# Pooling on token slices, and the next weights split behind the norms, in a two-layer encoder trunk on one core

## The chip, the cores and the metric

The kernel runs on one NeuronCore of a Trainium2 chip. TensorE (PE in the profile; PEld is its weight load) multiplies, VectorE (DVE), ScalarE (ACT) and GpSimd (POOL) work element by element, SyncE (SP) issues most of the transfers. The metric is the device time of one execution in microseconds; lower is better.

## The reference

528 tokens (16 learned meta tokens and 512 frames) of 1024 channels pass through two layers. Each layer is a half-step SwiGLU FFN, a token mixer and another half-step FFN, all with an RMS norm in front and a residual around. The mixer of the first layer is pooling, that of the second is latent attention.

```python
h = h + 0.5 * swiglu(rmsnorm(h, ffn1_norm[l]), ffn1_w_gate[l], ffn1_w_up[l], ffn1_w_down[l])
u = rmsnorm(h, mix_norm[l])
h = h + pool_mixer(u, pool_w[l], pool_scale[l])        # first layer
...
def pool_mixer(h, w_group, scale):
    # per group of 256 channels: mean over the last w tokens (w = 2, 4, 8, 16) minus the token,
    # then a 256 x 256 map per group, then a scale per channel
def swiglu(h, w_gate, w_up, w_down):
    return (jax.nn.silu(h @ w_gate) * (h @ w_up)) @ w_down     # 1024 -> 2816 -> 1024
```

All data is float32.

## The kernel before

**Layout.** Channels lie on the partitions: `h` is eight tiles of 128 channels by 528 tokens. Every product is made in three passes of a reduced-precision float format: an operand is split into a high part (ScalarE copies it) and a low part (VectorE subtracts the copy), and high x high, high x low and low x high are added up in PSUM. So each operand, weights too, costs one ScalarE and one VectorE instruction before TensorE can use it.

**Weights.** `fetch(u)` (line 162) brings one unit of 128 x 1024 into one of two buffers (`raw`) by SyncE's queue, copies it (L169) and subtracts (L170); `fetch_gate_up` (line 331) does so for the gate and the up unit of one chunk. `wide` tiles hold the parts, 14 of them.

**FFN.** The 2816 hidden channels are 22 chunks of 128. A *plain* chunk (`gate_up_plain`, `plain`, L371) is 8 k-tiles x 3 passes x 2 token halves x 2 (gate and up) = 96 matmuls. A *recursive* chunk (`gate_up`, `product`, L383) gets gate and up from 7 products of half the depth, 84 matmuls, out of sums of the weights and sums of the inputs. The weight sums are brought by `bring_sums` (two SyncE transfers and one accumulating GpSimd transfer, L401 to L403) and `bring`, added and split by `prepare` (L421, L422, L183, L184). The input sums are made by `sums_x(x, k)` (L245 to L248, then L183 and L184), one call for each pair of k-tiles. The first chunks of an FFN are plain: in the first, second and fourth FFN `first_chunks` runs five (`begun = 5`), in the third `first_chunk` runs two. Down products (L193) of a block of four chunks are handed out over the slots of the next block.

**Norms at an FFN's start.** In `first_chunks` chunk 0 and 1 are made from inputs that lack the norm's factor. `rms[0]()` makes the factor's columns, `rms[1]()` spreads them over the partitions (L303) and ScalarE copies them out (L307, L305). Then `normal_x` for each of eight k-tiles multiplies (L224, VectorE), copies the high part (L183, ScalarE) and subtracts (L184, VectorE). Chunk 2 takes the k-tiles one after the other (`by_chunk`). In the third FFN the inputs are normalised in the stage before it, between the products of the shared keys and values, and handed over as `x_1`.

**Pooling.** After the first FFN the residual `h` of a channel tile is written by VectorE (L617), split into `xm` (L210 ScalarE, L211 VectorE), squared (L262) and the square added to a running sum (L263, GpSimd mostly). `z_products` (L734) multiplies token tiles by the group's weights; `z_scale` makes the norm's factor per token, `z_parts` (L740, L741) scales and splits; band matrices then do the pooling over tokens (L766 to L778), L780 adds the residual, and the next FFN's input is split and squared. A band product over 256 or 272 output tokens needs earlier tokens too. Four token tiles are slices of 128; the tokens left over, 240 to 255 and 512 to 527, are gathered by GpSimd copies (L695) into a fifth tile of 80 rows (`x5`, `s5`), which has zeros between.

**Order.** The order of instructions on each engine is set when the kernel is built, by a planner that goes by the order of the program, by what is ready, and by estimated durations. An engine then works its list in order. `with tc.issue_after(i):` adds one constraint: instructions written inside the block for the engine of `i` come after `i` on that engine. Instructions of other engines are not bound.

Of the kernel before, what the change touches and what calls it, by code (L numbers as in the profile page):

```python
# [58 lines left out]
B_0, B_4, B_M, NB = 0, 256, 528, 928  # L59
# [21 lines left out]


def tail(ap):

    return ap.rearrange("p (a b) -> p a b", b=NM)[:, 15::17, :]


def spread(ap):

    return ap.rearrange("p (a b) -> p a b", b=64)[:, :, :NM]  # L90
# [3 lines left out]
def trunk(ctx: ExitStack, tc, h0, wall, vecs, band, rope, out):  # L94
# [24 lines left out]
    def unsplit():  # L119
        return rawp.tile([P, 1024], F32, tag="raw", name=name("raw"))  # L120

# [59 lines left out]
    def split_to(dst, src):  # L181

        nc.scalar.activation(dst[0], src, AF.Copy)  # L183
        nc.vector.tensor_tensor(dst[1], src, dst[0], op=ALU.subtract)  # L184
# [33 lines left out]
    def normal_x(xs, c, g, t0, r):  # L218
# [6 lines left out]
        if c >= KC // 2:  # L225
            p = slot(F32R)[:, :T], slot(F32R)[:, :T]
            split_to(p, xn)
            xs["b"][c] = [(p[0][:, a : a + n], p[1][:, a : a + n]) for a in (0, n)]
            return
# [101 lines left out]
    def fetch_gate_up(u0, one=fetch):  # L331
        one(u0)
        one(u0 + 1)

    def ffn(u0, x, g, rms, t0, after, early=None, final=None, normed=None, hooks=()):
# [56 lines left out]

        def pair_of_sums():
            return sump.tile([P, 2, 512], F32, tag="sum", name=name("sum"))
# [136 lines left out]
        def first_chunks():  # L531

            nonlocal x
# [16 lines left out]
            plain(w_g, pg, halves)  # L550
            r = rms[1]()
            fetch_gate_up(u0 + 6)
# [6 lines left out]
            fetch_gate_up(u0 + 9)  # L559
            sums_x(x, 0)  # L560
            gate_up_plain(2, True)
            fetch_gate_up(u0 + 12)
            sums_x(x, 1)
            sums_x(x, 2)
            gate_up_plain(3)
            bring_sums(5)
            bring(5)
            evacuate(0, *held, r)
            sums_x(x, 3)
            bring_sums(6)  # L570
            gate_up_plain(4, pair=True)
            prepare(5)
            bring(6)

        def first_chunk():
# [6 lines left out]
            for k in range(2):  # L582
                sums_x(x, k)
            gate_up_plain(1)
            for k in range(2, 4):
                sums_x(x, k)
            prepare(2)
# [38 lines left out]
        begun = 5 if normed is None else 2  # L626
# [42 lines left out]
    rows = [P, P, P, P, 80]  # L669
    x5, bands = [], []  # L670

    def early():
# [11 lines left out]
        for i in range(2):  # L684
            x5.append((slot(F32R)[:, :512], slot(F32R)[:, :512]))
            for t in x5[i]:
                nc.gpsimd.memset(t.bitcast(F32), 0.0)

    done = prep([(xm, V_MIX, 0)], ssq_m, 0)

    def after(c):
        done(c)
        for e in range(2):
            t = x5[c // 4][e][:, (c % 4) * P : (c % 4) * P + P]
            nc.gpsimd.tensor_copy(spread(t), tail(xm[c][e]))  # L695
# [5 lines left out]
    s5 = slot()[:, :P]  # L701
    nc.gpsimd.memset(s5, 0.0)
    nc.vector.tensor_copy(spread(s5), tail(ssq_m))

    def tokens(j, c, e):
        if j == 4:
            return x5[c // 4][e][:, (c % 4) * P : (c % 4) * P + 80]
        return xm[c][e][:, j * P : (j + 1) * P]

    def z_scale():  # L710

        ps = psum()
        for j in range(5):
            sj = s5[:, :80] if j == 4 else ssq_m[:, j * P : (j + 1) * P]
            nc.tensor.matmul(ps[: rows[j], 2 * j : 2 * j + 2], sj, ones_d, start=True, stop=True)
        v, rc = small(5), small(5)
        nc.vector.memset(v, 1.0)
        nc.vector.tensor_scalar(v[:, :4], ps[:, 0:8:2], EPS, None, op0=ALU.add)
        nc.vector.tensor_scalar(v[:80, 4:5], ps[:80, 8:9], EPS, None, op0=ALU.add)
# [17 lines left out]
    def z_parts(j, b, ps):  # L737
# [3 lines left out]
        nc.vector.scalar_tensor_tensor(zl, ps, rc[:n, j : j + 1], zh, op0=ALU.mult, op1=ALU.subtract)  # L741
        z[j][b] = zh, zl

# [7 lines left out]
    for j, b in ((1, 1), (2, 1), (3, 1), (4, 1)):  # L751
        z_parts(j, b, z_products(j, b, psum()))
# [530 lines left out]
```

## Time and profile before

| | |
|---|---|
| time, three runs | 1695.87, 1699.82, 1700.03 us (median 1699.82) |
| profiled execution | 1702.0 us, of which the profile's span is 1700.2 |
| mean granted clock of TensorE | 0.981 of full speed |
| busy, share of the span | TensorE 96%, VectorE 67%, ScalarE 48%, GpSimd 13% |
| matmuls | 11976 |

How to read it: a row of the timeline is an instruction (or several alike, x count) with its start, its duration, engine, line of the code, operation and shape; in square brackets stands how long the engine stood idle before it and what ended that. Durations of neighbours on one engine can overlap by some hundredths of a microsecond; the chain shows net times. Matmuls overlap by more, so their pitch is the length of a run of them over their count.

### The profile page before, as it was taken

The numbers are of one execution on the slowest core, as the hardware profiler recorded it, in microseconds if no ns is written. First come the engines' busy times: TensorE is split into PE (matmuls) and PEld (weight loads), VectorE is DVE, ScalarE is ACT, GpSimd is POOL, SyncE is SP. The second block draws the span as 40 slices with busy tenths as digits, with TensorE's granted clock in tenths as the row PEclk, the third lists the DMA queues.
The fourth block names the chain that finished last, engine by engine and source line by source line (L and its number), as shares of the span: only waits on it lengthen the run. The fifth ranks groups of instructions, "written<-read, shape, count | busy, mean of one in ns | idle before, by whom it ended". The sixth has DMA issues, their size and how long they took to land.

```text
span 1700.2 us, 30059 instructions
## 1 busy us (share of the span) xinstructions
PE 1637.3 (96%) x11976; PEld 1555.5 (91%) x11976; DVE 1142.5 (67%) x1851; ACT 809.5 (48%) x1489; POOL 221.9 (13%) x257
## 2 busy tenths in 40 slices
PE   7999999998999999999899999999899899999997
PEld 7899999997999999999899999898787798999897
DVE  6865666657776566657767667566787766666655
ACT  6543444446454444445454444445576453444443
POOL 2000000005200000002000000001454100000002
PEclk9999999997999999999999999999899899999998
DMA  7455465533244555534355565643102434565411
GB/s 250 112 137 149 139 160 139 141 111 109 75 113 137 148 146 136 138 101 149 88 135 150 153 145 152 152 126 111 50 14 75 124 96 132 142 160 148 134 56 61
DMA packets 166206, 212.20 MB, mean 125 GB/s; under 512 B 10288, under 2 KB 102576, under 8 KB 166064
## 3 DMA queue, kind: packets, MB, share of 16 engines
q1 hardware_dynamic: 146176, 172.60, 32.2%
q0 software_dynamic: 19312, 37.23, 13.3%
q8 instruction: 94, 1.54, 0.4%
q10 hardware_dynamic: 576, 0.43, 0.1%
q14 instruction: 48, 0.39, 0.1%
HBM read 208.12 MB, written 2.10 MB: 124 GB/s over the span
## 4 chain that ended last, share of the span: by engine, by line
PE 84%; DVE 8%; DMA 3%; ACT 3%; issue 1%; POOL 0%; SPq 0%; DVEq 0%; ACTq 0%; POOLq 0%
PE ps L383 41%; PE ps L193 32%; PE ps L371 7%; DMA raw<-wall 2%; DVE t L184 2%; DVE t L224 1%; DVE w L170 1%; PE ps L1065 1%; DMA half<-wall 1%; ACT w L183 1%; DVE w L184 1%; PE ps L978 1%; PE ps L734 0%; PE ps L933 0%; ACT t L990 0%
## 5 line engine op out<-in xcount | busy, mean ns | idle before, releaser
L383 PE MATMUL ps<-t,w 128*128 128x256 f32 (+1 forms) x5964 | 757.1, 283 | 7.9 <-ACT t L525 6.7
L383 PEld LDWEIGHTS ps<-t,w 128*128 128x128 f32 x5964 | 740.1, 188 | 21.0 <-ACT t L525 8.1
L193 PE MATMUL ps<-t,w 128*128 128x264 f32 (+2 forms) x3672 | 628.4, 322 | 6.6 <-ACT t L183 2.0
L193 PEld LDWEIGHTS ps<-t,w 128*128 128x128 f32 x3672 | 527.9, 188 | 54.3 <-ACT t L183 5.0
L183 ACT ACTIVATE w<-half 128x512 fp32r<-128x512 f32 (+1 forms) x263 | 154.6, 603 | 230.8 <-PE ps L383 122.4
L371 PE MATMUL ps<-t,w 128*128 128x264 f32 (+1 forms) x1632 | 222.0, 297 | 21.5 <-DVE t L184 10.1
L371 PEld LDWEIGHTS ps<-t,w 128*128 128x128 f32 x1632 | 211.7, 199 | 30.1 <-DVE t L184 15.0
L403 POOL DMA_DIRECT2D sum<-wall x71 | 86.2, 1215 | 1077.9 <-DMA sum<-wall 400.6
L183 ACT ACTIVATE w<-sum 128x1024 fp32r<-128x1024 f32 x142 | 149.9, 1057 | 161.1 <-PE ps L383 108.2
L184 DVE TENSOR_TENSOR w<-half,w 128x512 fp32r<-128x512 f32 (+1 forms) x263 | 168.4, 655 | 70.6 <-ACT w L183 69.0
L184 DVE TENSOR_TENSOR w<-sum,w 128x1024 fp32r<-128x1024 f32 x142 | 173.1, 1220 | 54.3 <-PE ps L383 36.8
L614 DVE SCALAR_TENSOR_TENSOR h<-ps,h 128x528 f32<-128x528 f32 (+1 forms) x160 | 111.6, 697 | 140.1 <-PE ps L193 139.8
L183 ACT ACTIVATE t<-t 128x528 fp32r<-128x528 f32 (+4 forms) x174 | 99.0, 593 | 115.8 <-DVE t L526 62.9
L521 DVE TENSOR_TENSOR t<-ps,t 128x256 f32<-128x256 f32 (+1 forms) x71 | 30.3, 427 | 139.4 <-PE ps L383 138.5
L184 DVE TENSOR_TENSOR t<-t,t 128x528 fp32r<-128x528 f32 (+4 forms) x174 | 109.3, 643 | 11.2 <-ACT t L183 9.9
L184 DVE TENSOR_TENSOR w<-raw,w 128x1024 fp32r<-128x1024 f32 x71 | 86.7, 1221 | 28.1 <-PE ps L383 20.5
L183 ACT ACTIVATE w<-raw 128x1024 fp32r<-128x1024 f32 x71 | 74.9, 1055 | 55.5 <-PE ps L383 26.0
L170 DVE TENSOR_TENSOR w<-raw,w 128x1024 fp32r<-128x1024 f32 (+1 forms) x52 | 67.3, 1297 | 22.7 <-ACT w L169 21.1
L169 ACT ACTIVATE w<-raw 128x1024 fp32r<-128x1024 f32 (+1 forms) x55 | 54.5, 994 | 54.3 <-DMA raw<-wall 23.1
L263 POOL TENSOR_TENSOR t<-t,t 128x528 f32<-128x528 f32 (+1 forms) x33 | 52.9, 1603 | 156.4 <-ACT t L262 99.1
L513 ACT ACTIVATE t<-ps 128x256 f32<-128x256 f32 (+1 forms) x71 | 27.3, 385 | 81.8 <-PE ps L383 81.2
L211 DVE SCALAR_TENSOR_TENSOR t<-h,vt,t 128x528 fp32r<-128x528 f32 (+1 forms) x48 | 52.2, 1107 | 6.3 <-ACT t L210 6.1
(167 smaller groups left out, 1080.5 us busy)
## 6 DMA issues: line engine op xcount, KB each, us to landing
raw<-wall SPq DMA_DIRECT2D x118, 512.0 KB, 3.4
half<-wall SPq DMA_DIRECT2D x199, 256.0 KB, 3.8
sum<-wall SPq DMA_DIRECT2D x142, 256.0 KB, 3.2
sum<-wall POOLq DMA_DIRECT2D x71, 512.0 KB, 7.0
half<-wall SPq DMA_DIRECT2D x64, 192.0 KB, 2.8
h<-h SPq DMA_DIRECT2D x8, 264.0 KB, 5.6
raw<-wall SPq DMA_DIRECT2D x8, 256.0 KB, 4.0
raw<-band SPq DMA_DIRECT2D x4, 464.0 KB, 4.1
```

The source lines that it names most:

```text
L169: nc.scalar.activation(wh[:, a:b], raw[:, a:b], AF.Copy)
L170: low.tensor_tensor(wl[:, a:b], raw[:, a:b], wh[:, a:b], op=ALU.subtract)
L183: nc.scalar.activation(dst[0], src, AF.Copy)
L184: nc.vector.tensor_tensor(dst[1], src, dst[0], op=ALU.subtract)
L193: nc.tensor.matmul(ps, w[a], x[b][:, c0:c1], start=first and n == 0, stop=last and n == 2)
L211: nc.vector.scalar_tensor_tensor(xl, src, gain(g + c), xh, op0=ALU.mult, op1=ALU.subtract)
L263: (nc.vector if last else nc.gpsimd).tensor_tensor(ssq, ssq, sq, op=ALU.add)
L371: nc.tensor.matmul(ps, w[a][:, k * P : k * P + P], xs[k][i][b], start=k == 0 and n == 0, stop=k == KC - 1 and n == 2,)
L383: nc.tensor.matmul(ps, w[a][:, k * P : k * P + P], xs[k][b], start=first and k == 0 and n == 0, stop=last and k == 3 and n == 2, skip_grou ...
L403: nc.gpsimd.dma_start(t, up[:, :512].unsqueeze(1).to_broadcast([P, 2, 512]), accum_op=ALU.add)
L521: add(u[:, first], pd, u[:, first], op=ALU.add)
L614: nc.vector.scalar_tensor_tensor(hv, at, 0.5, hv, op0=ALU.mult, op1=ALU.add)
```

## The change

Pooling uses five slices of the token axis, 0 to 128, 128 to 256, 240 to 368, 368 to 496 and 496 to 528, with no gathered tile: the fifth has 32 rows, the copies, zeroed tiles and `s5` go, and the band matrices are 16 columns wider. The two fetches for the second FFN's first chunk are written inside a block behind the last low part of z. In `first_chunks` the factor is spread after six of the eight k-tiles of chunk 1's gate, the weights and input sums from chunk 3 on are written behind the low part of the last norm, and six chunks are plain instead of five (`begun = 6`). In `first_chunk` (third FFN) the sums and `prepare(2)` are written behind the last norm.

```diff
-B_0, B_4, B_M, NB = 0, 256, 528, 928
+B_0, B_4, B_M, NB = 0, 256, 528, 944
...
     def split_to(dst, src):
 
-        nc.scalar.activation(dst[0], src, AF.Copy)
-        nc.vector.tensor_tensor(dst[1], src, dst[0], op=ALU.subtract)
+        return (
+            nc.scalar.activation(dst[0], src, AF.Copy),
+            nc.vector.tensor_tensor(dst[1], src, dst[0], op=ALU.subtract),
+        )
...
-            split_to(p, xn)
+            _, xs["low"] = split_to(p, xn)
...
-            plain(w_g, pg, halves)
+            plain(w_g, pg, halves, range(6))
             r = rms[1]()
+            plain(w_g, pg, halves, range(6, KC))
             fetch_gate_up(u0 + 6)
             xs = new_x()
             for c in range(KC):
...
             x = xs
-            fetch_gate_up(u0 + 9)
-            sums_x(x, 0)
-            gate_up_plain(2, True)
-            fetch_gate_up(u0 + 12)
-            sums_x(x, 1)
-            sums_x(x, 2)
-            gate_up_plain(3)
-            bring_sums(5)
-            bring(5)
-            evacuate(0, *held, r)
-            sums_x(x, 3)
-            bring_sums(6)
-            gate_up_plain(4, pair=True)
-            prepare(5)
-            bring(6)
+            with tc.issue_after(xs["low"].ins):
+                fetch_gate_up(u0 + 9)
+                sums_x(x, 0)
+                gate_up_plain(2, True)
+                fetch_gate_up(u0 + 12)
+                sums_x(x, 1)
+                sums_x(x, 2)
+                gate_up_plain(3)
+                fetch_gate_up(u0 + 15)
+                sums_x(x, 3)
+                gate_up_plain(4)
+                evacuate(0, *held, r)
+                bring_sums(6)
+                bring(6)
+                bring_sums(7)
+                gate_up_plain(5, pair=True)
+                prepare(6)
+                bring(7)
...
             bring_sums(2)
             bring(2)
-            for k in range(2):
-                sums_x(x, k)
-            gate_up_plain(1)
-            for k in range(2, 4):
-                sums_x(x, k)
-            prepare(2)
+            with tc.issue_after(x["low"].ins):
+                for k in range(2):
+                    sums_x(x, k)
+                gate_up_plain(1)
+                for k in range(2, 4):
+                    sums_x(x, k)
+                prepare(2)
...
-        begun = 5 if normed is None else 2
+        begun = 6 if normed is None else 2
...
-    rows = [P, P, P, P, 80]
-    x5, bands = [], []
+    spans = [(0, P), (P, 2 * P), (240, 368), (368, 496), (496, L)]
+    rows = [b - a for a, b in spans]
+    bands = []
...
-        for i in range(2):
-            x5.append((slot(F32R)[:, :512], slot(F32R)[:, :512]))
-            for t in x5[i]:
-                nc.gpsimd.memset(t.bitcast(F32), 0.0)
-
-    done = prep([(xm, V_MIX, 0)], ssq_m, 0)
-
-    def after(c):
-        done(c)
-        for e in range(2):
-            t = x5[c // 4][e][:, (c % 4) * P : (c % 4) * P + P]
-            nc.gpsimd.tensor_copy(spread(t), tail(xm[c][e]))
+
+    after = prep([(xm, V_MIX, 0)], ssq_m, 0)
...
-    s5 = slot()[:, :P]
-    nc.gpsimd.memset(s5, 0.0)
-    nc.vector.tensor_copy(spread(s5), tail(ssq_m))
-
     def tokens(j, c, e):
-        if j == 4:
-            return x5[c // 4][e][:, (c % 4) * P : (c % 4) * P + 80]
-        return xm[c][e][:, j * P : (j + 1) * P]
+        return xm[c][e][:, slice(*spans[j])]
...
     for j, b in ((1, 1), (2, 1), (3, 1), (4, 1)):
-        z_parts(j, b, z_products(j, b, psum()))
-
-    fetch(U_FFN2_0, 2)
-    fetch(U_FFN2_0 + 1, 2)
+        low = z_parts(j, b, z_products(j, b, psum()))
+
+    with tc.issue_after(low.ins):
+        fetch(U_FFN2_0, 2)
+        fetch(U_FFN2_0 + 1, 2)
...
-        b_2, b_3 = bm[:, P : P + 272], bm[:, :272]
-        b_4 = b04[:80, B_4 : B_4 + 272]
+        b_2, b_3 = bm[:, P + 16 : P + 288], bm[:, 16:288]
+        b_4 = b04[: rows[4], B_4 : B_4 + 272]
...
-        b[:, g, B_M : B_M + 400] = entries(s, np.arange(-P, 272)[None], w, True)
-        src = np.full(P, -1000)
-        src[:16] = np.arange(240, 256)
-        src[64:80] = np.arange(512, 528)
-        b[:, g, B_4 : B_4 + 272] = entries(src[:, None], np.arange(256, 528)[None], w, True)
+        b[:, g, B_M : B_M + 416] = entries(s, np.arange(-P, 288)[None], w, True)
+        b[:, g, B_4 : B_4 + 272] = entries(s + 496, np.arange(256, 528)[None], w, True)
```

## Rows read from the trace of the kernel before

**Rows 1.** The page's first part: busy time, share of the span, instructions.

```profile
PE 1637.3 (96%) x11976; PEld 1555.5 (91%) x11976; DVE 1142.5 (67%) x1851; ACT 809.5 (48%) x1489; POOL 221.9 (13%) x257
```

**Rows 2.** Stretches: length, each engine's busy time (instructions), granted clock, DMA share, GB/s.

```profile
37.76:61.74 23.98, 18.86 (x112) 17.02 (x113) 22.67 (x46) 11.93 (x19) 1.24 (x1) 0.86 0.47 133
382.65:418.20 35.55, 27.55 (x166) 25.71 (x167) 27.52 (x36) 20.43 (x32) 20.43 (x25) 0.76 0.36 115
448.92:491.35 42.43, 41.92 (x338) 41.23 (x338) 39.20 (x72) 20.73 (x39) 2.44 (x2) 1.00 0.36 88
817.53:839.57 22.04, 16.85 (x103) 15.04 (x102) 21.97 (x48) 7.89 (x19) 1.23 (x1) 0.85 0.29 73
1342.44:1357.98 15.54, 11.08 (x45) 8.10 (x45) 15.54 (x35) 6.25 (x13) 0.00 (x0) 0.74 0.45 102
```

**Rows 3.** Timeline of TensorE in two undisturbed stretches of plain matmuls.

```profile
466.91 24.60 PE L371 MATMUL ps<-t,w 128*128 128x264 f32 x200 [0.23 <-DVE t L184]
...
1316.65 11.49 PE L371 MATMUL ps<-t,w 128*128 128x256 f32 x96
```

**Rows 4.** The chain that ended last, 40 to 60 us: start, net us, what.

```profile
39.67 0.68 DVE t L184 x2
40.35 0.68 DVE t L224
...
43.88 1.13 DVE w L170
...
49.76 0.34 DVE t L247
```

**Rows 5.** VectorE's groups by shape, 33.95 to 56.6 us: busy, mean ns | idle before.

```profile
L170 DVE TENSOR_TENSOR w<-raw,w 128x1024 fp32r<-128x1024 f32 x4 | 4.9, 1221 | 2.6 <-ACT w L169 2.6
...
L245 DVE TENSOR_TENSOR t<-t 128x264 f32<-128x264 f32 x4 | 1.7, 425 | 0.0
```

**Rows 6.** Timeline of the first FFN's start, ScalarE, and its first recursive products.

```profile
32.68 0.58 ACT L307 ACTIVATE t<-ps 128x512 f32<-128x512 f32 x1
...
34.95 1.06 ACT L169 ACTIVATE w<-raw 128x1024 fp32r<-128x1024 f32 x1 [1.62 <-DMA raw<-wall]
35.92 0.72 ACT L183 ACTIVATE t<-t 128x264 fp32r<-128x264 f32 x2
...
82.79 11.85 PE L383 MATMUL ps<-t,w 128*128 128x264 f32 x96
```

**Rows 7.** Timeline of the fourth FFN's start, ScalarE and VectorE.

```profile
1336.82 0.60 ACT L307 ACTIVATE t<-ps 128x512 f32<-128x512 f32 x1
...
1339.15 0.69 DVE L421 TENSOR_TENSOR sum<-sum,raw 128x512 f32<-128x512 f32 x1 [3.45 <-DMA raw<-wall]
...
1341.62 1.41 DVE L224 SCALAR_TENSOR_TENSOR t<-h,vt,t 128x512 f32<-128x512 f32 x2
```

**Rows 8.** Timeline of the third FFN's start, VectorE and ScalarE.

```profile
816.89 2.35 DVE L184 TENSOR_TENSOR w<-sum,w 128x1024 fp32r<-128x1024 f32 x2
...
817.51 0.57 ACT L307 ACTIVATE t<-ps 128x512 f32<-128x512 f32 x1
```

**Rows 9.** VectorE's and GpSimd's groups by shape, about 382 to 418 us.

```profile
L211 DVE SCALAR_TENSOR_TENSOR t<-h,vt,t 128x528 fp32r<-128x528 f32 x8 | 8.6, 1093 | 1.3 <-ACT t L210 1.3
L170 DVE TENSOR_TENSOR w<-raw,w 128x1024 fp32r<-128x1024 f32 x4 | 6.7, 1678 | 0.3 <-ACT w L169 0.3
...
L695 POOL CAST t<-t 128x32 fp32r<-128x32 f32 x16 | 10.3, 658 | 21.9 <-ACT t L210 19.7 <-DVE t L211 2.1
```

**Rows 10.** The chain that ended last, 380 to 420 us.

```profile
391.00 3.32 DMA raw<-wall
...
394.42 1.06 ACT w L169
```

**Rows 11.** Timeline of VectorE in the band loop.

```profile
422.80 0.75 DVE L211 SCALAR_TENSOR_TENSOR t<-h,vt,t 128x528 fp32r<-128x528 f32 x1
...
430.95 0.88 DVE L780 SCALAR_TENSOR_TENSOR h<-ps,vt,h 128x256 f32<-128x256 f32 x2
```

More of the change, by code (lines that the diff above doesn't have):

```diff
@@ L80 @@
 """
[L83 to L90, printed above, removed]
 @with_exitstack
@@ L120, in unsplit, with pair_of_sums @@
         return rawp.tile([P, 1024], F32, tag="raw", name=name("raw"))
+    def pair_of_sums():
+        return sump.tile([P, 2, 512], F32, tag="sum", name=name("sum"))
     def psum():
@@ L328, in prep, with fetch_gate_up @@
         return after
-    def fetch_gate_up(u0, one=fetch):
-        one(u0)
-        one(u0 + 1)
+    def fetch_gate_up(u0):
+        fetch(u0)
+        fetch(u0 + 1)
     def ffn(u0, x, g, rms, t0, after, early=None, final=None, normed=None, hooks=()):
@@ L390, in product @@
                     )
-        def pair_of_sums():
-            return sump.tile([P, 2, 512], F32, tag="sum", name=name("sum"))
         def bring_sums(f):
@@ L713, in z_scale @@
         for j in range(5):
-            sj = s5[:, :80] if j == 4 else ssq_m[:, j * P : (j + 1) * P]
-            nc.tensor.matmul(ps[: rows[j], 2 * j : 2 * j + 2], sj, ones_d, start=True, stop=True)
-        v, rc = small(5), small(5)
+            nc.tensor.matmul(ps[: rows[j], 2 * j : 2 * j + 2], ssq_m[:, slice(*spans[j])], ones_d, start=True, stop=True)
+        v, rc, n = small(5), small(5), rows[4]
         nc.vector.memset(v, 1.0)
         nc.vector.tensor_scalar(v[:, :4], ps[:, 0:8:2], EPS, None, op0=ALU.add)
-        nc.vector.tensor_scalar(v[:80, 4:5], ps[:80, 8:9], EPS, None, op0=ALU.add)
+        nc.vector.tensor_scalar(v[:n, 4:5], ps[:n, 8:9], EPS, None, op0=ALU.add)
         for a, b in ((0, 2), (2, 5)):
@@ L740, in z_parts @@
         nc.scalar.activation(zh, ps, AF.Copy, scale=rc[:n, j : j + 1])
-        nc.vector.scalar_tensor_tensor(zl, ps, rc[:n, j : j + 1], zh, op0=ALU.mult, op1=ALU.subtract)
+        low = nc.vector.scalar_tensor_tensor(zl, ps, rc[:n, j : j + 1], zh, op0=ALU.mult, op1=ALU.subtract)
         z[j][b] = zh, zl
+        return low
     two = psum_pair()
```

## The prediction

> **What bounds the kernel now.** The page's busy line comes first: TensorE holds a matmul for 96% of the span and no other engine comes near [rows 1]. So the run is a row of matmuls, and what can change is the number of matmuls, the places where they wait, and the clock there. The matmul pitch is read from two undisturbed stretches: 200 of 264 columns in 24.60 us and 96 of 256 columns in 11.49 us [rows 3], 0.122 and 0.119 us each. With that pitch the table by stretches shows where time goes lost: matmuls counted in a stretch, times the pitch, against its length [rows 2].
>
> Start of the first FFN, from its by-chunk matmuls on: 112 x 0.122 = 13.7 of 23.98 us, 10.3 lost. Pooling, from its first product to its band matmuls: 166 x 0.120 = 19.9 of 35.55 us, 15.6 lost. Start of the second FFN: 338 x 0.122 = 41.2 of 42.43 us, 1.2 lost. Start of the third (the one with normalised input at hand): 103 x 0.12 = 12.4 of 22.04 us, 9.6 lost. Start of the fourth: 45 x 0.119 = 5.4 of 15.54 us, 10.2 lost. Together 47 us (a few records may be missing from the counts; a missing per cent makes a stretch's loss 0.1 to 0.4 smaller). Part of it is not waiting but the lower clock that follows: the mean granted clock of four of these stretches is 0.74 to 0.86 [rows 2], so some of the time was spent at 1.2 GHz instead of 2.4, after TensorE had stood still in short pieces. Remove the standstill and that part goes too.
>
> Then the chain of the first start: from 39.7 us on it is VectorE nearly alone [rows 4]. A token tile's norm costs 0.68 us, its two low parts 0.68, together 1.36. TensorE uses 12 matmuls on a tile, 1.46 us. So norms alone would feed it. They don't come alone: between them stand weight splits of 1.13 us and the sums' steps of 0.34 [rows 4]; in the whole stretch 4 splits, and 14 such steps in four groups of which one is shown [rows 5]. That is 4.5 + 4.8 us, and with an early preparation (sums and one split, 2.3) some 11.6 us in the norms' way, against 10.3 lost.
>
> **The change, part by part.**
> *Splits and sums behind the last norm (three FFNs that normalise at their start).* The order on VectorE changes, not its work. In the first FFN the factor is spread and copied by 33.3 [rows 6]. With the spread moved ahead of 12 of the 48 gate matmuls it is there 1.5 us earlier, 31.8. Eight norms at 1.36 end at 42.7, with ScalarE's turn between about 43.7. The up matmuls of chunk 1 keep TensorE until 37.8 as before (the same matmuls stand in another order), and it wants the last tile 7 x 1.46 later, at 48.0: no wait is left. All 10.3 us could come back; I take 9.0, since ScalarE's high part stands in a queue with weight copies, bounds 4 and 10.3. The next weights must be split by 37.8 + 11.7 = 49.5 us; VectorE begins them at 43.7 and needs 2.3 for two. That cover is 3 us; without it TensorE would wait for every microsecond beyond. In the fourth FFN the factor is copied from 1336.82 on, but VectorE stands at an addition that waited 3.45 us for a transfer, and the first norm begins at 1341.62 [rows 7]. Both go behind the norms: I take 9.2 of 10.2, bounds 4 and 10.2. In the second there is little to win: 0.5 of 1.2, bounds -2 (its VectorE now also carries splits deferred from pooling) and 1.2.
>
> ScalarE is the weak point. In the trace a weight copy waits 1.62 us for its transfer at 34.95, and the norm's high part starts only at 35.92, behind it [rows 6]. The Trainium skill (TensorE: Matmul & The Clock Gate, Architectural detail) says that ScalarE and VectorE are strict first-in-first-out; that speaks against putting a long tail behind one instruction, since whatever waits there holds everything. By that rule a copy placed before a norm would cost its wait, 1.6 us at each of three starts, and the time would be some 5 us longer than the result below, still inside the bounds taken; I give it a sixth of the forecast's chance. The trace agrees with the rule.
>
> The queues behind: the order binds VectorE alone, transfers stay in SyncE's queue, but there are two buffers for unsplit units, and a buffer is free only after its low part. So the transfer of chunk 4's gate unit, which used to start in the norms, now waits for chunk 3's low part at about 45, takes 3.32 and a copy of 1.06 [rows 10], and is split near 51; it is wanted at 37.8 + 2 x 11.7 = 61.2. What stands behind it in SyncE's queue are the sums' transfers for chunks 6 and 7, wanted after 84; GpSimd's accumulating transfers follow those. One recursive chunk less also means one set of sums' transfers less a start, for two plain units more. None of that is priced.
>
> *The third FFN.* Its factor is ready at 818.1, and two splits of 2.35 us together run into that moment [rows 8]. They and others now come after the norms, but there is no extra chunk to hide them: VectorE was busy 21.97 of 22.04 us of the stretch [rows 2], and the same work has to be done before the sums' products. TensorE starts earlier and then waits later. Gain 2.5, bounds +7 (the tail fits) and -4 (three splits, 3.5, that had run while the factor was made are now fully in the way).
>
> *Six plain chunks.* A plain chunk is 96 matmuls, a recursive one 7 products of 12, so 84. Three FFNs (not the third) have one more: 36 x 0.12 = 4.3 us lost. It buys VectorE 11.7 us in each start. From 43.7 it has to do, in the first FFN, six splits (6.8), four pairs of tiles' sums (each 4 x 0.34 + 2 x 0.68 at most, 10.9), five closings of chunks (an estimate, four operations of 0.34 to 0.68, 2 each, 10) and one preparation (three and a half splits and two additions of half a split, 5.1): done at 77, and the first recursive chunk, at 82.79 now [rows 6], would begin at 37.8 + 4 x 11.7 = 84.6. Spare 7 us. The down products of block 0 crowd into four slots instead of six; they are matmuls that alternate with others, no price.
>
> *Pooling.* Gone are 16 copies on GpSimd (10.3 us of its time in this stretch), its five memsets and a copy. GpSimd keeps its additions of squares. VectorE has eight low parts of 1.09 us mean there, and four full weight splits of 1.68 [rows 9]; alone they take 0.75 [rows 11] and 1.13 [rows 4]. The splits leave for behind the last low part of z, and so does the blocking on ScalarE, whose weight copy came after a transfer of 3.32 us that the chain runs through [rows 10]. What stays is a true chain: last residual, its two parts, squares, z's scale, z's parts. I let it cost 5 of the 15.6: gain 10.5, bounds 4 (the chain was the wait anyway) and 15.6. The tile of 32 instead of 80 rows costs the same: as many matmuls of as many columns. Deferred are four half splits (2.3 us) before the next FFN's first use. In the band loop VectorE needs 0.88 for two residuals and 0.75 to 1.09 for the low part [rows 9, 11], 1.8 a tile, against 11 matmuls, 1.34. It falls behind by 8 x 0.46 + 2.3 = 6.0 us, but the FFN takes its tiles one per 1.46 us, and needs the last one 10 us after the first: covered. Without that cover 6.0 us would show. The band rows grow by 16 columns in 928: nothing.
>
> The page SBUF - State Buffer of the Trainium skill (Who interferes with whom) says that a VectorE instruction with two SBUF inputs and a GpSimd instruction that reads SBUF exclude each other for their whole length. The trace agrees in direction: 1.09 against 0.75, but copies that only move data are not told from additions there. By that rule GpSimd's additions, which stay, would keep about half of the 8 x 0.34 us in place, and the time would be about 1 us longer; the value above does without it.
>
> **Sum.** 9.0 + 0.5 + 2.5 + 9.2 + 10.5 - 4.3 = 27.4 us. The profiled execution took 1702.0 us (span 1700.2), so 1674.6; it lies 2.2 above the median of the runs shown, so 1672 as a median. All lower bounds give 1.7 us of gain (1698), all upper ones 40 (1660).
>
> **Rivals.**
> A, the wait moves on: behind the norms each pair of splits waits for its transfer and copy (3.32 and 1.06, [rows 10]), and VectorE idles meanwhile, 13 us over three pairs. It would be done at 90 instead of 77, over 5 us late for the first recursive chunk, at three starts; and the third start loses 4 instead of winning 2.5. 1672 + 15 + 6.5 = 1694. For it: only two buffers for unsplit weights. Against: sums stand in the same queue and fill the gaps.
> B, pooling's own chain: the splits were in the shadow of residual, square and scale; gain 4, not 10.5: 1679. For it: the additions on GpSimd stay. Against: transfers and splits lead the chain there [rows 10].
> C, slower: VectorE, not its order, is the bound. Then no start gains, each split that ran in idle time before a factor arrived (three of 1.13 and the sums' addition before them in the third start, 4.8, and one in the first, 1.2) is added, and 4.3 for matmuls: 1699.8 + 10.3 = 1710. It decides if the last norm's low part is no earlier, relative to the factor, than now. Against: the count above, 11.6 us of foreign work in the norms' way.
> D, the planner's order hardly moves: 4.3 lost, nothing won, 1704.
>
> **Chances.** Forecast 0.62; B 0.18; A 0.12; C 0.04; D 0.04. The likeliest stays 1672. Range 1661 to 1690: it holds B and most of the forecast's own bounds, and leaves out A, C, D and the fully recovered end. A measurement tells about 0.3%, 5 us, from no change; A lies on that edge. Faster 0.88, same 0.07, slower 0.05.
>
> **What would show it.** No weight split and no sums' step between the first and the last norm in three starts; matmul counts over length near the pitch there, and full clock; the first recursive chunk starting without a wait; 36 matmuls more in plain chunks; pooling from first product to band matmuls in about 25 us instead of 35.55, with no copy on GpSimd. Wrong would be: TensorE waiting for VectorE at the first recursive product, ScalarE's copies before the norms, or band tiles that VectorE can't close in time.

## The result and the profile after

The changed kernel takes 1672.64 us (median of four runs, 1670.08 to 1674.3) against 1698.65 for the kernel before: ratio 0.9848, 95% interval 0.9829 to 0.9867, so 1.3 to 1.7% faster, 26.0 us by the medians. The forecast was 1672. The profiled execution took 1672.39 us, with a span of 1670.1 and a mean granted clock of 0.995 instead of 0.981. Its busy line, which answers to [rows 1]:

```profile
PE 1622.6 (97%) x12012; PEld 1544.4 (92%) x12012; DVE 1128.5 (68%) x1832; ACT 802.5 (48%) x1471; POOL 209.8 (13%) x233
```

36 matmuls more, as counted, and less time. Cut at marks that both kernels have (the start of a stage's first matmul on TensorE; the second FFN up to its last recursive product, the fourth up to the end of the last matmul), the two profiled executions differ as follows. The forecast has the 36 matmuls in it, 1.4 us in each of three FFNs.

| stretch | before | after | difference | forecast |
|---|---|---|---|---|
| first FFN, up to pooling's first product | 382.65 | 376.03 | -6.6 | -7.6 |
| pooling, first product to first band matmul | 35.55 | 22.98 | -12.6 | -10.5 |
| band loop, to the next FFN's first matmul | 10.81 | 13.67 | +2.9 | 0 |
| second FFN, to its last product | 351.64 | 352.34 | +0.7 | +0.9 |
| shared keys' stage, third FFN, attention | 536.00 | 533.52 | -2.5 | -2.5 |
| fourth FFN and end | 376.95 | 364.78 | -12.2 | -7.8 |
| sum | 1693.60 | 1663.32 | -30.3 | -27.5 |

The executions differ by more than the medians, since the profiled one of the kernel before lies 3.4 us above its median. So a total that fits holds one stretch that was put at nothing and lost 2.9 us, two that were sized too small, and one, the fifth line, that fits by chance, as shown below. The stretches of the kernel after (columns as in [rows 2]) are the first start, pooling, the band loop, the third start and the fourth start.

```profile
31.50:54.69 23.19, 23.19 (x191) 23.19 (x191) 20.31 (x40) 12.17 (x21) 0.00 (x0) 1.00 0.20 70
376.03:399.01 22.98, 20.85 (x168) 19.72 (x167) 18.19 (x26) 15.12 (x26) 11.27 (x8) 1.00 0.08 26
399.01:412.68 13.67, 13.67 (x91) 11.29 (x89) 13.65 (x26) 10.28 (x16) 4.00 (x3) 1.00 0.32 113
...
803.54:833.28 29.74, 28.75 (x216) 27.54 (x216) 27.51 (x60) 14.66 (x30) 2.24 (x1) 0.94 0.16 46
1298.54:1370.59 72.05, 71.00 (x593) 70.18 (x592) 56.81 (x94) 37.30 (x66) 8.29 (x6) 1.00 0.41 125
```

Two things are to be seen. The granted clock is 1.00 in four of the lines and 0.94 in the third start, where [rows 2] had 0.74 to 0.86 in these three starts and in pooling. And the first line holds 191 matmuls in 23.19 us, 0.121 each, the pitch of [rows 3]: no wait is left in the first start. The third line's 91 matmuls, in contrast, keep TensorE busy all the time and still take 0.150 each: no wait, but slow matmuls.

The order in the first start, from the timeline of VectorE:

```profile
31.99 1.45 DVE L219 SCALAR_TENSOR_TENSOR t<-h,vt,t 128x528 f32<-128x528 f32 x2 [0.92 <-ACT t L300]
...
43.34 0.76 DVE L219 SCALAR_TENSOR_TENSOR t<-h,vt,t 128x528 f32<-128x528 f32 x1
44.88 0.71 DVE L178 TENSOR_TENSOR t<-t,t 128x528 fp32r<-128x528 f32 x1 [0.77 <-ACT t L177]
45.50 0.77 DVE L450 TENSOR_TENSOR t<-ps,t 128x264 f32<-128x264 f32 x2
46.19 1.22 DVE L163 TENSOR_TENSOR w<-raw,w 128x1024 fp32r<-128x1024 f32 x1
```

The norms run from 31.99 to 45.59 without a weight split between them, and the first split follows at 46.19. The forecast had the factor at 31.8 and the end at 43.7: the last four tiles are split in one piece instead of halves, and three of them take 2.1 us each, because VectorE waits 0.71 to 0.77 for ScalarE's high part. The wanted time was 48.0, so it cost nothing here.

In what follows, two numbers tell how far a single profile can be trusted. The attention stage, written alike in all kernels of this study, took from 141.24 to 144.40 us in the profiles of the changed kernel and its twelve variants, and the first start, in those that share it, from 78.54 to 80.52. Both go with the granted clock. Attention took 141.24 to 141.97 us where it was 0.99, 142.27 to 142.39 at 0.98 and 143.62 to 144.40 at 0.96; the first start took 78.54 to 79.12 us at 1.00 and 80.30 to 80.52 at 0.98. The attention stage before, and then after:

```profile
1172.68:1316.65 143.97, 134.91 (x707) 113.13 (x706) 110.67 (x251) 91.82 (x204) 69.07 (x111) 0.96 0.16 52
1157.01:1298.54 141.53, 132.07 (x708) 110.75 (x707) 111.31 (x252) 91.81 (x204) 70.52 (x111) 0.99 0.15 53
```

So 2.4 of the table's 30.3 us are scatter of this kind. Totals of single executions therefore say little below 3 us; stretches around an edit say more.

### The profile page after: what moved, and what is told of

Its sections match the earlier page's. It is cut to its first block, busy times and chain, and to the rows that moved or that the text cites. A ratio compares the mean times of both kernels' runs of the same rounds, so it can differ in the third digit from the quotient of the medians.

```text
span 1670.1 us, 30002 instructions
## 1 busy us (share of the span) xinstructions
PE 1622.6 (97%) x12012; PEld 1544.4 (92%) x12012; DVE 1128.5 (68%) x1832; ACT 802.5 (48%) x1471; POOL 209.8 (13%) x233
## 4 chain that ended last, share of the span: by engine, by line
PE 87%; DVE 6%; ACT 3%; DMA 2%; issue 1%; POOL 0%; SPq 0%; DVEq 0%; ACTq 0%; POOLq 0%
PE ps L378 39%; PE ps L188 31%; PE ps L366 12%; DMA half<-wall 1%; DVE t L178 1%; DVE t L206 1%; PE ps L1049 1%; ACT w L177 1%; DVE w L178 1%; DVE t L219 1%; ACT t L177 1%; PE ps L962 1%; DVE h L615 1%; DVE w L163 1%; ACT t L974 0%
## 5 line engine op out<-in xcount | busy, mean ns | idle before, releaser
L378 PE MATMUL ps<-t,w 128*128 128x256 f32 (+1 forms) x5712 | 726.5, 283 | 9.5 <-ACT t L517 5.7
L366 PE MATMUL ps<-t,w 128*128 128x264 f32 (+1 forms) x1920 | 242.7, 288 | 10.2 <-ACT w L162 5.3
L177 ACT ACTIVATE w<-sum 128x1024 fp32r<-128x1024 f32 x136 | 143.5, 1058 | 160.6 <-PE ps L378 116.6
L395 POOL DMA_DIRECT2D sum<-wall x68 | 82.1, 1208 | 1052.9 <-DMA sum<-wall 464.9
L178 DVE TENSOR_TENSOR w<-sum,w 128x1024 fp32r<-128x1024 f32 x136 | 165.7, 1220 | 29.4 <-PE ps L378 16.9
L178 DVE TENSOR_TENSOR w<-raw,w 128x1024 fp32r<-128x1024 f32 x68 | 83.1, 1222 | 28.0 <-PE ps L378 21.5
L162 ACT ACTIVATE w<-raw 128x1024 fp32r<-128x1024 f32 (+1 forms) x61 | 60.7, 1000 | 57.4 <-DMA raw<-wall 37.3
L163 DVE TENSOR_TENSOR w<-raw,w 128x1024 fp32r<-128x1024 f32 (+1 forms) x58 | 72.5, 1257 | 7.4 <-ACT w L162 6.7
```

The source lines that it names most:

```text
L162: nc.scalar.activation(wh[:, a:b], raw[:, a:b], AF.Copy)
L163: low.tensor_tensor(wl[:, a:b], raw[:, a:b], wh[:, a:b], op=ALU.subtract)
L177: nc.scalar.activation(dst[0], src, AF.Copy),
L366: nc.tensor.matmul(ps, w[a][:, k * P : k * P + P], xs[k][i][b], start=k == 0 and n == 0, stop=k == KC - 1 and n == 2,)
L378: nc.tensor.matmul(ps, w[a][:, k * P : k * P + P], xs[k][b], start=first and k == 0 and n == 0, stop=last and k == 3 and n == 2, skip_grou ...
L395: nc.gpsimd.dma_start(t, up[:, :512].unsqueeze(1).to_broadcast([P, 2, 512]), accum_op=ALU.add)
```

## Experiments

All variants start from the changed kernel. Ratios are to the kernel before, run on the same chip.

**The band loop: how many rows.** Three variants replace the 32-row tile by a slice that overlaps the one ahead of it; band rows of tokens covered twice are zero.

```diff
-    spans = [(0, P), (P, 2 * P), (240, 368), (368, 496), (496, L)]
+    spans = [(0, P), (P, 2 * P), (240, 368), (368, 496), (400, L)]
...
-        b[:, g, B_4 : B_4 + 272] = entries(s + 496, np.arange(256, 528)[None], w, True)
+        late = np.where(s + 400 < 496, -1000, s + 400)
+        b[:, g, B_4 : B_4 + 272] = entries(late, np.arange(256, 528)[None], w, True)
```

> The changed kernel, but the last token tile is a slice of 128 tokens (400 to 528) instead of 32 (496 to 528); band rows of tokens that an earlier slice already covers are zero, so nothing of the result changes. Theory S (each change between a matmul of 128 rows and one of 32 rows costs TensorE about 0.2 us beyond the pitch, and the band loop has 16 such changes): the stretch from the first band matmul to the next FFN's first matmul falls from 13.67 to about 10.7 us, and the time from 1672.6 to 1669.7. Theory V (VectorE, with residuals, low parts and the four late half splits, sets the band loop): the stretch stays within 0.4 of 13.67 and the time within 0.5 of 1672.6.

With 448 and 464 in place of 400, the tile has 80 and 64 rows:

> As the run with 128 rows, but the last slice is 80 tokens (448 to 528), as many rows as the gathered tile before the change had. Theory S says that it is not the shortness but a small number of rows: before, 80 rows showed 0.12 us net a matmul, so the band loop is about 10.7 us again. If any tile shorter than 128 costs a change, it stays near 13.7. Theory V: near 13.7.

> As the run with 128 rows, but the last slice is 64 tokens (464 to 528). If the cost of a change is bound to matmuls that use half of the rows or less, the band loop stays near 13.7 us; if it is bound to 32 rows alone, it falls to about 10.7; if the cost grows with the number of unused rows, it lies between (about 12.7).

Band loop: 13.67 us with 32 rows, 13.68 with 64, 10.78 with 80, 10.71 with 128. Theory S holds for the stretch, and the limit lies between 64 and 80 rows. The timeline of TensorE around the fifth tile's two matmuls (L761, L762), with 32 rows:

```profile
408.58 0.29 PE L760 MATMUL ps<-t,t 128*128 128x272 f32 x1
408.80 0.39 PE L761 MATMUL ps<-t,t 32*128 32x272 f32 x1
409.03 0.28 PE L762 MATMUL ps<-t,t 32*128 32x272 f32 x1
409.25 0.39 PE L750 MATMUL ps<-t,t 128*128 128x256 f32 x1
409.47 0.28 PE L751 MATMUL ps<-t,t 128*128 128x256 f32 x1
```

with 64 rows:

```profile
405.53 0.39 PE L761 MATMUL ps<-t,t 64*128 64x272 f32 x1
405.76 0.28 PE L762 MATMUL ps<-t,t 64*128 64x272 f32 x1
405.97 0.39 PE L750 MATMUL ps<-t,t 128*128 128x256 f32 x1
```

and with 80:

```profile
404.57 0.29 PE L761 MATMUL ps<-t,t 80*128 80x272 f32 x1
404.70 0.28 PE L762 MATMUL ps<-t,t 80*128 80x272 f32 x1
404.83 0.28 PE L750 MATMUL ps<-t,t 128*128 128x256 f32 x1
```

What counts is the distance of starts. From 408.58 to 409.47 are four steps of 0.22 to 0.23, in place of 0.12 to 0.13: 0.4 us in each of eight passes, some 3 us.

But the time hardly moved: 1671.98 us, ratio 0.9848 (0.9827 to 0.9868), as without the edit (with 80 rows 1671.46 and with 64 rows 1672.94, two runs each). The second FFN's start became longer, 75.25 instead of 72.73. The timeline of TensorE with 128 rows:

```profile
409.92 5.25 PE L366 MATMUL ps<-t,w 128*128 128x264 f32 x40
416.28 7.68 PE L366 MATMUL ps<-t,w 128*128 128x264 f32 x56 [1.10 <-DVE t L206]
```

After 40 matmuls the fifth input tile isn't there, and the next 56, with short waits among them at the next tiles, take 0.137 each. VectorE's timeline says why:

```profile
408.89 1.55 DVE L163 TENSOR_TENSOR w<-raw,w 128x1024 fp32r<-128x1024 f32 x1
...
412.53 1.94 DVE L163 TENSOR_TENSOR w<-raw,w 128x1024 fp32r<-128x1024 f32 x1
...
415.20 5.22 DVE L206 SCALAR_TENSOR_TENSOR t<-h,vt,t 128x528 fp32r<-128x528 f32 x4
```

Two splits of chunk 1's weights stand between the input tiles. With 32 rows they stand there too; the slow matmuls only let VectorE keep up. Rival V was wrong for the loop and, within the noise, right for the time.

**Chunk 1's splits behind the input tiles.** In the second FFN alone, with `low` the last input tile's low part; once with 128 rows, once with the 32 of the change:

```diff
-            fetch_gate_up(u0 + 3)
+            with tc.issue_after(low.ins):
+                fetch_gate_up(u0 + 3)
```

> The run with a last slice of 128 tokens, and in the second FFN alone the fetches of chunk 1's weights are written behind the low part of its last input tile. Theory M (with 128 rows the band loop itself gives 2.95 us, but then TensorE waits at the fifth input tile, because VectorE splits chunk 1's two weight units, 1.5 and 1.9 us, before the tiles): the start of the second FFN goes from 75.25 back to about 72.7 us with the band loop at 10.7, and the time from 1671.98 to 1669.4. Rival W (VectorE has too much work in this stretch in any order): another wait of about 2.5 us shows up before the first recursive product of the second FFN, the time stays within 0.5 of 1672.

> The changed kernel with its 32-row tile, and chunk 1's weights of the second FFN behind the last input tile, as in the run before it. Theory M: nothing to win alone, because the 32-row matmuls slow TensorE by as much as VectorE lags: band loop 13.7, start of the second FFN 72.7, time within 0.5 of 1672.6. Rival (the late splits also cost the band loop): 1670.0.

Band loop and second start together: 86.39 us in the changed kernel, 85.96 with 128 rows, 86.35 with the late splits alone, 84.40 with both. So alone the edits win 0.4 us and nothing, and both win 2.0 of the 3 us. The rest went to a smaller wait. TensorE, with both:

```profile
413.06 11.85 PE L367 MATMUL ps<-t,w 128*128 128x264 f32 x96
...
425.76 1.36 PE L367 MATMUL ps<-t,w 128*128 128x264 f32 x9
427.96 1.24 PE L367 MATMUL ps<-t,w 128*128 128x264 f32 x8 [0.84 <-ACT t L539]
```

and ScalarE:

```profile
426.57 1.06 ACT L163 ACTIVATE w<-raw 128x1024 fp32r<-128x1024 f32 x1 [7.71 <-DMA raw<-wall]
427.53 1.22 ACT L539 ACTIVATE t<-ps 128x264 f32<-128x264 f32 x4
```

No input tile is waited for any longer: 96 matmuls run through. But the two buffers for unsplit weights come free later, the next weight copy stands ahead of the emptying of PSUM, and both wait for the transfer. As a whole, no gain can be told: 1673.32 us, ratio 0.9851 (0.9836 to 0.9866). With 32 rows and late splits it is 1672.84, 0.9851 (0.9827 to 0.9874).

A third variant keeps the gate unit where it was and moves only the up unit, `fetch(u0 + 4)`, with 128 rows.

> A slice of 128 tokens, and in the second FFN only the up unit of chunk 1 is fetched behind the last input tile (the run before had both units there: the 1.10 us wait was gone, but a new one of 0.84 stood behind a ScalarE copy that waited for a transfer, since the buffers came free later). Theory M: both waits gone, band loop 10.7, start of the second FFN 72.7, so 83.4 for the two against 86.4 in the changed kernel and 84.4 with both units late; time 1669.7. Rival W (any order leaves VectorE short there): the two stretches together stay at 84.4 or above.

The two stretches took 11.27 + 74.14 = 85.41 us, above 84.4, as the rival said: a wait of 1.06 on a residual of VectorE took the place of the 1.10. It ran 1671.65 us, ratio 0.9843 (0.9829 to 0.9856): the lowest median of the versions timed four times or more, and still not told from the changed kernel.

**Pooling: slices or order.** First the gathered tile of 80 rows comes back, and the fetches stay behind z; then the slices stay, and the fetches are free.

```diff
+        for e in range(2):
+            t = x5[c // 4][e][:, (c % 4) * P : (c % 4) * P + P]
+            nc.gpsimd.tensor_copy(spread(t), tail(xm[c][e]))
```

> The changed kernel with the gathered fifth tile of 80 rows of before (its GpSimd copies, zeroed tiles and band matrices), while the fetches for the second FFN stay behind the last low part of z. Theory G (the gather's 10.3 us of GpSimd's time slow VectorE's low parts and stand in the chain to z, so the slices are worth about half of pooling's gain): pooling from first product to band matmuls 29 instead of 22.98 us, band loop 10.8, start of the second FFN 75.2; time 1672.6 + 6 - 0.4 = 1678. Rival F (the fetches' place is all that counts): pooling 23 to 24 us, time 1672 to 1673.5.

```diff
-    with tc.issue_after(low.ins):
-        fetch(U_FFN2_0, 2)
-        fetch(U_FFN2_0 + 1, 2)
+    fetch(U_FFN2_0, 2)
+    fetch(U_FFN2_0 + 1, 2)
```

> The changed kernel with its slices, but the two fetches for the second FFN's first chunk free to run before z's last low part. Theory F (copies that wait 3.32 us for a transfer and four half splits stand in pooling's chain): pooling 28 to 35 us instead of 22.98, less up to 2.3 that VectorE no longer does in the band loop; time 1676 to 1683. Rival G (without the gather the chain has room for them): pooling 23 to 24.5, time 1672 to 1674.

Gather back: 1680.01 us, 0.9896 (0.9883 to 0.9910), pooling 30.53. Fetches free: 1678.88, 0.9888 (0.9874 to 0.9901), pooling 30.18. The changed kernel has 22.98, the one before 35.55. Taking out one part costs 7.2 to 7.6 us of the 12.6; by the same numbers, each part put in alone would bring the kernel before only 5.0 to 5.4. So the two stalls overlap: while one is left, the chain starts late. VectorE's groups by shape in pooling, with the gather:

```profile
L216 DVE SCALAR_TENSOR_TENSOR t<-h,vt,t 128x528 fp32r<-128x528 f32 x8 | 7.1, 904 | 2.3 <-ACT t L215 2.1
...
L268 DVE TENSOR_TENSOR t<-t,t 128x528 f32<-128x528 f32 x1 | 0.7, 709 | 4.6 <-POOL t L268 4.6
```

with the fetches free:

```profile
L206 DVE SCALAR_TENSOR_TENSOR t<-h,vt,t 128x528 fp32r<-128x528 f32 x8 | 10.1, 1277 | 0.9 <-ACT t L205 0.9
L163 DVE TENSOR_TENSOR w<-raw,w 128x1024 fp32r<-128x1024 f32 x4 | 6.0, 1496 | 0.4 <-ACT w L162 0.4
...
L163 DVE TENSOR_TENSOR w<-raw,w 128x512 fp32r<-128x512 f32 x4 | 3.1, 794 | 0.0
```

and in the changed kernel:

```profile
L206 DVE SCALAR_TENSOR_TENSOR t<-h,vt,t 128x528 fp32r<-128x528 f32 x8 | 10.4, 1332 | 2.1 <-ACT t L205 2.1
```

With the gather, the last addition of squares (L268) waits 4.6 us for GpSimd, whose additions queue behind its copies. With the fetches free, VectorE carries 9.1 us of splits in this stretch: the four halves and, behind them in the queue, four whole ones. The low parts themselves are no part of the gain: 1.33 us each in the changed kernel, above the 1.09 of before.

Most of the loss is clock. In both variants TensorE's waits in pooling are only some 2.6 us longer than in the changed kernel (4.7 and 4.6 against 2.1), but the granted clock is 0.78 with the gather and 0.83 with the fetches free, where the changed kernel has 1.00:

```profile
376.20:406.80 30.60, 25.75 (x168) 24.78 (x168) 16.25 (x28) 16.01 (x28) 15.61 (x25) 0.78 0.07 24
376.20:406.80 30.60, 26.04 (x170) 23.88 (x169) 26.70 (x35) 21.12 (x34) 12.08 (x8) 0.83 0.38 130
```

**The three starts: order, plain chunks, spread.** The first variant drops the block.

```diff
-            with tc.issue_after(xs["low"].ins):
-                fetch_gate_up(u0 + 9)
-                sums_x(x, 0)
+            fetch_gate_up(u0 + 9)
+            sums_x(x, 0)
...
```

> The changed kernel without the block in the three starts (weights and input sums from chunk 3 on are free again to stand between the norms); six plain chunks and the earlier spread stay. Theory O (the order is what brings the starts' gain): the prediction's 9.0 + 0.5 + 9.2 come back but for what the earlier spread gives, 1.5 each in two of them: 1672.6 + 15.7 = 1688. Rival R (the sixth plain chunk and the earlier factor are enough, the order adds little): 1672 to 1675.

1691.94 us, 0.9957 (0.9943 to 0.9972). Up to the first product the first start took 87.09 us (80.30 in the changed kernel), the second 75.90 (72.73), the fourth 81.58 (72.06): 19.5 together. Theory O holds, and its 15.7 was low. TensorE in the first start shows the old picture of [rows 2]:

```profile
42.88 1.73 PE L366 MATMUL ps<-t,w 128*128 128x264 f32 x12 [0.48 <-DVE t L178]
45.67 2.10 PE L366 MATMUL ps<-t,w 128*128 128x264 f32 x12 [1.05 <-DVE t L178]
```

Twelve matmuls and a wait for the next tile; behind each wait the twelve take longer than 1.46. Then five plain chunks, the order kept:

```diff
-                fetch_gate_up(u0 + 15)
-                sums_x(x, 3)
-                gate_up_plain(4)
+                bring_sums(5)
+                bring(5)
...
-        begun = 6 if normed is None else 2
+        begun = 5 if normed is None else 2
```

> The changed kernel with five plain chunks instead of six in the three starts (the second to fourth FFN's sums as before the change), the order behind the last norm kept. Theory P (the sixth plain chunk pays): 36 matmuls fewer give back 4.3 us, but the first recursive chunk stands 11.7 us earlier, and VectorE, by the prediction's sum done at 77 against 72.9, is 4 us late at each of three starts: 1672.6 - 4.3 + 12 = 1680. Rival Q (VectorE has that much slack at its place): 1668.3.

1683.64 us, 0.9914 (0.9898 to 0.9929): theory P. Start and products together, the three FFNs are 3.5, 3.7 and 3.1 us longer although they have 1.4 less to do: 4.9 late each, where 4 was expected. TensorE at the first recursive products:

```profile
72.46 5.64 PE L378 MATMUL ps<-t,w 128*128 128x264 f32 x45
81.04 0.59 PE L378 MATMUL ps<-t,w 128*128 128x264 f32 x1 [2.95 <-ACT t L177]
```

Last, the spread behind all eight k-tiles again:

```diff
-            plain(w_g, pg, halves, range(6))
+            plain(w_g, pg, halves)
             r = rms[1]()
-            plain(w_g, pg, halves, range(6, KC))
```

> The changed kernel with the norm's factor spread after all eight k-tiles of chunk 1's gate, as before the change. Theory L (with the order behind the norms the tiles come faster than TensorE takes them, so a factor 1.5 us later costs little): each start within 0.3 us, time 1672 to 1673.5. Rival E (the earlier factor is needed to keep TensorE supplied): 1.5 us at each of three starts, time 1677.

1676.35 us, 0.9872 (0.9855 to 0.9889), near rival E by the time, with an interval that overlaps that of the changed kernel. By stretches it is mixed: the first start 80.56 instead of 80.30, the second 72.84 instead of 72.73, only the fourth 73.45 instead of 72.06. There TensorE meets the tiles:

```profile
1332.69 0.74 PE L366 MATMUL ps<-t,w 128*128 128x256 f32 x4 [0.22 <-DVE t L178]
1334.01 0.50 PE L366 MATMUL ps<-t,w 128*128 128x256 f32 x2 [0.58 <-ACT t L177]
1334.74 0.74 PE L366 MATMUL ps<-t,w 128*128 128x256 f32 x4 [0.22 <-DVE t L178]
```

The last tiles come every 2.05 us, and TensorE has six matmuls for each here, some 0.7 us, so the spread's lead is used up there. In the changed kernel only the last two of these waits are left, 0.58 at 1329.11 and 0.22 behind it. The waits are 1.0 of the 1.4 us longer. The first FFN's products (1.8) and attention (2.1) make up most of the rest of that profile. Attention's part goes with its granted clock of 0.96; whether the spread has a part in the products stays open.

**The third start.** The block in `first_chunk` goes, nothing else.

```diff
-            with tc.issue_after(x["low"].ins):
-                for k in range(2):
-                    sums_x(x, k)
-                gate_up_plain(1)
+            for k in range(2):
+                sums_x(x, k)
+            gate_up_plain(1)
```

> The changed kernel without the block in the third FFN's start: input sums and the first preparation are free again to run while the norm's factor is made. Theory T (the third start has no spare chunk, so what is put behind the norms comes back as waits before the first recursive products): its start gets longer by about 2.5 us, the stretch of recursive chunks shorter by about 4.3, net 1.8, so 1670.8. Rival, the prediction's own step (the order gains 2.5 there and the later loss has another cause): 1675.1. Rival N: TensorE is fed alike by both orders and the time stays within 0.5 of 1672.6.

1675.06 us, 0.9866 (0.9847 to 0.9886): slower by 2.4, near the rival's 1675.1, though the interval overlaps that of the changed kernel. The stretches decide. Without the block the shared keys' stage is 40.35 instead of 38.52 us, the start 32.27 instead of 29.74, the products 321.70 instead of 323.73: -1.8, -2.5 and +2.0, a gain of 2.3 for the block. Theory T fell. Of the products' loss that it rested on, 4.3 us, the block makes 2.0, and that doesn't eat the gain, since the block also pays in the stage ahead of it, where the norms stand. The other 2.3 are there without the block too (321.70 us against 319.40 in the kernel before), and what makes them was not tried.

## Why the prediction was right, and where not

*First start: right.* Forecast 9.0. The first recursive product came at 85.58 instead of 82.79 with 96 matmuls, 11.7 us, more ahead of it: 8.9 (forecast 84.6, without a wait; it came without one). The changed kernel's profile has the slower kind of first start, at a clock of 0.98, so with the quicker kind it would be up to 1.8 more. About 1 us is lost again among the products (9.25 us shorter, with 84 matmuls fewer, 10.2); its cause was not tried.

*Second start: right in sum, for another reason.* The order is worth 3.2 there (the variant without it), not 0.5, but against the kernel before the FFN wins only 0.7. That VectorE brings its lag along from the band loop would explain it; no run tries that by itself.

*Third start: the order right, the sum luck.* 2.5 forecast, 2.3 by the run without the block. Part of it lies in a stretch that the prediction had not named. But against the kernel before nothing is left: the shared keys' stage, the start and the products took 40.36, 32.27 and 319.40 us and take 38.52, 29.74 and 323.73, the same together. The step "TensorE starts earlier and then waits later" holds, and the later loss was sized too small. The -2.5 in the table is attention, which the change doesn't touch.

*Fourth start: the mechanism right, the term too small.* From the start of the FFN to the first product it went from 72.82 to 72.06 us with 11.5 of matmuls more, so 12.3 were won against a forecast of 9.2. (Another 1.4 lie among the products and were not traced.) The stretch of [rows 2] ended at 1357.98, as if the loss did. The windows of the kernel before show the rest, behind the last long wait and behind 1357.98:

```profile
1353.43:1389.47 36.04, 35.53 (x256) 34.35 (x257) 26.68 (x46) 17.16 (x30) 1.20 (x1) 0.86 0.23 59
1357.98:1389.47 31.49, 31.49 (x244) 31.49 (x245) 22.13 (x36) 15.90 (x28) 1.20 (x1) 0.91 0.26 68
```

256 matmuls at a granted clock of 0.86 take 36.04 us where the pitch makes 30.5: some 5.5 lost, mostly to the slower clock. Half of it lies inside the counted stretch; the second line, with a clock of 0.91 and no wait, holds some 2.5 that were not counted (244 matmuls at the pitch make 29.0 of 31.49). After the first start the clock had been back at 1.00 by 61.74, so that the mistake showed only here. Its size is partly chance: in the kernel before, TensorE's clock was at 1.2 GHz here from 1349.8 to 1363.6, 13.8 us, and in the variant without the order, behind waits of the same kind, for 10.2 us.

*Six plain chunks: right.* Priced at 4.3 us for VectorE's time. Without them the three FFNs lose 10.3.

*Pooling: right within its bounds, one reason wrong.* 12.6 against 10.5. That the low parts would fall from 1.09 to 0.75 is refuted: they are 1.33. What paid is fewer instructions ahead of z's squares on VectorE and GpSimd, and with them the clock, 1.00 instead of 0.76. The Trainium skill (SBUF - State Buffer, Who interferes with whom) has VectorE instructions with two SBUF inputs and GpSimd instructions that read SBUF exclude each other; the trace agrees. In the changed kernel two low parts run with nothing on GpSimd beside them and take 0.77 and 0.76 us; the six that overlap an addition take 1.14 to 1.83.

```profile
377.38 0.76 DVE L206 SCALAR_TENSOR_TENSOR t<-h,vt,t 128x528 fp32r<-128x528 f32 x1
381.31 4.68 DVE L206 SCALAR_TENSOR_TENSOR t<-h,vt,t 128x528 fp32r<-128x528 f32 x3
378.81 10.10 POOL L258 TENSOR_TENSOR t<-t,t 128x528 f32<-128x528 f32 x6 [57.65 <-ACT t L257]
```

With the gather it is the copies that are held up, as far as GpSimd's rough spans tell: one takes 0.68 us beside a low part and 0.2 without, and the additions queue behind them.

```profile
380.98 0.68 POOL L703 CAST t<-t 128x32 fp32r<-128x32 f32 x1
388.91 0.35 POOL L703 CAST t<-t 128x32 fp32r<-128x32 f32 x2
```

*The step that failed: "The tile of 32 instead of 80 rows costs the same: as many matmuls of as many columns."* It cost 2.96 us in the band loop, as the run with 128 rows shows. The Trainium skill has a rule for it (TensorEngine Tiling (Array Packing), Tiling Modes, Key Properties): a change of the tiling mode drains TensorE. The trace fits it, if a matmul of 32 or 64 rows between matmuls of 128 is such a change: steps of 0.22 us instead of 0.12 around each change between 32 or 64 rows and 128, none with 80. The drain itself is seen in no row.

*The cover was half right.* The band loop's "6.0 us, covered" did hold, but because the slow matmuls gave VectorE time. Without them TensorE waits 1.10 us at the fifth tile and more behind it, 2.5 together. The two mistakes hid each other: mending either one alone gives 0.4 us at most.

*Rival A* did not come: in the first start the copies behind the norms waited for their transfers, 2.50 and 1.45 us at 50.79 and 53.30, but sums filled VectorE's time. One copy did stand before the first norm's high part, at 32.21, a sign that the prediction had named; VectorE waited 0.18 us for it. Rival A's mechanism was seen where splits were moved once more, at 426.57 above: a weight copy that waits for a transfer holds the emptying of PSUM behind it. *B* is refuted by the run with the fetches free, which loses 7.2 us in pooling. *C and D* are excluded by the run without the order, which loses 19 us.

## What to carry to other kernels

An order on the busiest helper engine pays where TensorE takes its output piece by piece: put all that is wanted later behind the last piece, and buy the time for it with plain work on TensorE. Price a loss until the clock is back, not until the last wait ends. Before a slow step is mended, ask which engine is next late there: here 3 us of slow matmuls covered 2.5 us of VectorE's lag, and removing either alone was worth 0.4 us at most. Even both, 2.0 us in these stretches, could not be told in the time.

## What was not expected of the hardware

Matmuls of 32 or 64 rows between matmuls of 128 rows cost 0.2 us a change, also where TensorE never waits; 80 rows cost nothing.

The clock after a wait of the same kind differs between executions. Before pooling's last 24 products TensorE waits for z's parts: 1.69 us in the changed kernel's profile, after which the window shows

```profile
396.09:399.01 2.92, 2.92 (x24) 2.82 (x25) 2.92 (x5) 2.49 (x5) 0.00 (x0) 1.00 0.00 0
```

and 1.78 us in that of the variant with the late up unit:

```profile
396.26:400.73 4.47, 4.47 (x24) 4.47 (x25) 3.99 (x6) 2.66 (x5) 0.00 (x0) 0.62 0.00 0
```

The same 24 matmuls, 1.55 us apart by a granted clock of 1.00 or 0.62, that is, with all of the stretch at 2.4 GHz or much of it at 1.2. Part of the scatter between runs may come from there; that wait is the largest left in pooling.
